# Attention scores in a two-layer trunk: the second pass of the latents' scores on 64 rows, two heads at once

## The chip, the core and the metric

The kernel runs on one core of a Trainium2 chip. A core has a matrix engine (TensorE, "PE" in the profile, with its weight loads as "PEld"), a vector engine (VectorE, "DVE"), an activation engine (ScalarE, "ACT"), GpSimd ("POOL") and a queue that issues DMAs (SyncE, "SP"). The metric is the device time of one execution in microseconds. Before the change it was 1450.35 us, the median of 3 runs (1449.66 to 1453.91).

## The reference

Two layers of a trunk over 512 latent tokens, with a context of 256 tokens that goes through the same weights (the last layer drops the context's own output). Each layer has softmax attention (8 query heads of 64, 2 key heads), gated linear attention (GLA) and a gated MLP over chunks (SGU), merged by gates and normalised. The change is in the attention:

```python
def attend(q, k, v):
    s = jnp.einsum('btgrd,blgd->bgrtl', q, k, preferred_element_type=jnp.float32) * (ATTN_HEAD_DIM ** -0.5)
    p = jax.nn.softmax(s, axis=-1)
    return jnp.einsum('bgrtl,blgd->btgrd', p.astype(v.dtype), v)
...
    k_all = jnp.concatenate([kc, kl], axis=1)
    y_attn = blocked_attention(ql, k_all, v_all) * jax.nn.silu(a_g)
```

A latent query sees 256 + 512 = 768 keys, a context query the 256 of the context. All inputs are float32.

## The kernel before

TensorE takes float32 in a short form (F32R) in one pass, or in full in two. The kernel keeps the precision by splitting a number x into a high part (x rounded to F32R) and a low part (the rest), and by adding up products of the parts. Most matmuls of the kernel are such triples: high by high, high by low, low by high (`mm3`), written as three instructions with 256 to 512 columns.

The scores use the 128 rows of the array in another way. A head has only 64 numbers, so `queries` writes a head's high part and low part side by side (tile `qs`, 128 wide), transposes that (tile `qT`, in which rows 0 to 63 hold the high part and rows 64 to 127 the low part), and the keys' transposed tile `kT` holds each key twice, in the upper and in the lower 64 rows; `kT[:, g, 0]` are the keys' high parts and `kT[:, g, 1]` their low parts. One matmul against `kT[:, g, 0]` then gives (high + low) of the query by the high part of the key; a second one against `kT[:, g, 1]`, which accumulates in the same PSUM tile `s`, adds (high + low) by the low part.

The work is cut into items (t, g, pr): a tile t of 128 queries (t = 0, 1 the context, in layer 0 alone; t = 2 to 5 the latents), a key head g, and a pair pr of the four query heads that share it. For a latent item `scores` takes two PSUM tiles `s` (all there are of that tag), one for each head, and for each head two chunks of keys (512 and 256 columns) by two passes: eight matmuls. Then VectorE takes the negated row maximum (`sm<-s`), ScalarE the exponential with its sum (`P<-s,sm`), VectorE the reciprocal and the product; `values` transposes P on TensorE (`pt<-ident,P`, in full float32), splits it (`PTs`), and multiplies it by the values (`pt<-PTs,V`). There are 4 x 2 x 2 = 16 latent items in each of the two layers, and 8 context items in layer 0.

What stands around it: no engine's order is written by hand. Every operation is recorded with an estimated cost; a list scheduler (`Sched.order`) plays the whole program through with those costs, 16 times with changed priorities, and the order of the shortest plan is issued, engine by engine. So projections of the same layer (rows `p<-...`) are put between the pieces of the attention wherever TensorE would wait, and any changed cost can move instructions anywhere. `sc.group` records several matmuls as one operation with one cost: so far it served the GLA's masks (`s<-M`), 64 x 32 pieces of the array that are addressed by `tile_position`. Some elementwise operations may go to VectorE or GpSimd (`tta`), as the plan finds it cheaper.

Lines of the profile are those of helpers: L421 is the helper that records nearly every operation, L128 the one for operations with a choice of engine, L119 that of `sc.group`. Operations are told apart by their tiles.

Of the kernel before, what the change touches and what calls it, by code (L numbers as in the profile page):

```python
# [10 lines left out]
F32R = mybir.dt.float32r  # L11
I32 = mybir.dt.int32
AF = mybir.ActivationFunctionType
ALU = mybir.AluOpType
# [487 lines left out]
def kernel(ctx: ExitStack, tc: tile.TileContext, A, out, dbg=None):  # L502
    nc = tc.nc
    sc = Sched(nc)
    ACT, DVE, POOL, PE, SP = sc.ACT, sc.DVE, sc.POOL, sc.PE, sc.SP
# [8 lines left out]
    def T(tag, shape, dt=F32, name=None):  # L514
        return sc.tile(sb, shape, dt, tag, BUFS.get(tag, 1), name or tag, "SB")
# [14 lines left out]
    def act(out, in_, func=AF.Copy, **kw):  # L530
        return ACT.activation(out=out, in_=in_, func=func, **kw)
# [12 lines left out]
    def f(ap):  # L544
        return ap.bitcast(F32)
# [5 lines left out]
    identr = C([128, 128], F32R, name="identr")  # L551
# [14 lines left out]
    def tta(out, in0, in1, op):  # L566
        k = dict(out=out, in0=in0, in1=in1, op=op)
        return sc.alt((DVE, "tensor_tensor", k), (POOL, "tensor_tensor", k))
# [19 lines left out]
    LEVELS, SWITCH_PE = [[1, 2], [3, 4], [5, 6], [7]], 87.0  # L588
# [118 lines left out]
    def layer(l, X, start=None):  # L707
# [42 lines left out]
        q = T("T4", [128, 6, 8, 64], name="q")  # L750
        kT = T("T5", [128, 2, 2, NT], F32R, name="kT")
# [78 lines left out]
        for hf in range(2):  # L830
            wt = wgroup(w_in, 8, C_GV + 272 * hf, 272)
            for t in all_t:
                ps = tm(wt, 0, 272, X, t)
# [14 lines left out]
        for w, c0 in ((0, C_GK), (1, C_GQ)):  # L848
            wt = wgroup(w_in, 8, c0, 256)
            for pr in range(2):  # L850
                for seg in (["l", "c"] if (full or w == 0) else ["l"]):
                    ps = cm(wt, 128 * pr, 128, X, seg)
# [24 lines left out]
        for hf in range(2):  # L877
            wt = wgroup(w_in, 8, C_SV + 256 * hf, 256)
            for i, t0 in enumerate((2, 4, 0) if full else (2, 4)):
                g = T("F3", [128, 2, 256], name="keep")  # L880
# [13 lines left out]
        qTs = {}  # L894

        def queries(t, g):
            s = T("Q2", [128, 4, 2, 64], F32R, name="qs")
            act(s[:, :, 0], q[:, t, 4 * g:4 * g + 4])
            tta(s[:, :, 1], q[:, t, 4 * g:4 * g + 4], f(s[:, :, 0]), ALU.subtract)
            ps = PS("pt", [128, 4, 128], F32R)  # L900
            for h in range(4):
                PE.transpose(ps[:, h], s[:, h].rearrange("p a d -> p (a d)"), identr)
            qt = T("Q2", [128, 4, 128], F32R, name="qT")
            act(qt, f(ps))
            qTs[t, g] = qt

        def scores(t, g, pr):

            if pr == 0:
                queries(t, g)  # L910
            nk = (2 if t < 2 else 6) * 128
            sm = T("sm", [128, 16])
            if t < 2:
                S = [PS("s", [128, 2, 256])]
                P = [T("S3", [128, 2, 256], name="P")]
                heads = [(S[0][:, hh], P[0][:, hh]) for hh in range(2)]
            else:
                S = [PS("s", [128, 1, nk]) for _ in range(2)]
                P = [T("S3", [128, 1, nk], name="P") for _ in range(2)]
                heads = [(S[hh][:, 0], P[hh][:, 0]) for hh in range(2)]  # L920
            for hh, (s, p) in enumerate(heads):
                for c0 in range(0, nk, 512):
                    c1 = min(c0 + 512, nk)
                    for w in range(2):
                        PE.matmul(s[:, c0:c1], qTs[t, g][:, 2 * pr + hh], kT[:, g, w, c0:c1], start=(w == 0), stop=(w == 1))
            n = 2 // len(S)
            for i in range(len(S)):
                sc.bias -= SB
                DVE.tensor_reduce(out=sm[:, n * i:n * i + n], in_=S[i], axis=AX.X, op=ALU.max, negate=True)
                sc.bias += SB  # L930
                for hh in range(n * i, n * i + n):
                    act(heads[hh][1], heads[hh][0], AF.Exp, bias=sm[:, hh:hh + 1], accum_out=sm[:, 2 + hh:3 + hh])
                r = sm[:, 4 + n * i:4 + n * i + n]
                DVE.reciprocal(r, sm[:, 2 + n * i:2 + n * i + n])
                if n == 1:
                    sc.alt((DVE, "tensor_scalar", dict(out=P[i][:, 0], in0=P[i][:, 0], scalar1=r, scalar2=None, op0=ALU.mult)),
                           (POOL, "tensor_tensor", dict(out=P[i][:, 0], in0=P[i][:, 0], in1=r.to_broadcast([128, nk]), op=ALU.mult)))
                else:
                    tta(P[i], P[i], r.unsqueeze(2).to_broadcast([128, n, nk]), ALU.mult)
            return [p for _, p in heads]  # L940
# [48 lines left out]
        for grp in DECAYS:  # L989
            eg = {}  # L990
            for d, pr in grp:
                e = T("S3", [128, NT], name="ez")
                g = T("S3", [128, NT], name="gz")
                eg[d, pr] = e, g
                bias = gab[:, d, pr:pr + 1]
                for c0, c1 in ((0, 512), (512, 768)):
                    ps = PS("pt", [128, c1 - c0])
# [5 lines left out]
            for d, pr in grp:  # L1003
                e, g = eg[d, pr]
# [15 lines left out]
        for pr in range(2):  # L1020
# [17 lines left out]
            for c0, c1 in ((0, 4), (4, 6)):  # L1038
                u = PS("s", [128, 2 * (c1 - c0), 128])
                for c in range(c0, c1):  # L1040
# [5 lines left out]
                    for hh in range(2):  # L1046
                        h = 2 * pr + hh
# [4 lines left out]
            for d, seq in ((0, [0, 1, 2, 3, 4, 5]), (1, [1, 0, 5, 4, 3, 2])):  # L1052
                r = slice(64 * d, 64 * d + 64)
# [16 lines left out]
            for gi in range(2):  # L1070
# [4 lines left out]
                for lvs in LEVELS:  # L1075
                    ps = PS("s", [128, 2, 512])
                    calls, kq, views, off, cost = [], [], {}, 0, SWITCH_PE
                    for lv in lvs:
# [23 lines left out]
                        w = 64 if lv in (1, 7) else 32  # L1102
                        views[lv] = ps[:, :, off:off + ng * w].rearrange("p h (c j) -> p h c j", c=ng)
                        off += ng * w
                        for ci in range(ng):
                            for hh in range(2):
                                r = slice(64 * hh, 64 * hh + 64)
# [36 lines left out]
                ps = PS("s", [128, nu, 128])  # L1144
                for j in range(nu):
                    ci, hh = j // 2, j % 2
                    c, h = g0 + ci, 2 * pr + hh
# [67 lines left out]
        for t in q_t:  # L1215
# [7 lines left out]
            ps = PS("pt", [128, 4, 128])  # L1223
# [3 lines left out]
        for b in range(4):  # L1227
            g = T("S3", [128, NQ], name="kept")
# [290 lines left out]
    with tc.manual_schedule():  # L1519
        a = 0  # L1520
# [73 lines left out]
```

## Time and profile before

| | before |
|---|---|
| median of 3 runs | 1450.35 us |
| the profiled execution: its time | 1449.78 us |
| its span on the core | 1448.0 us |
| TensorE busy | 1397.2 us (96%) |
| TensorE weight loads busy | 1232.3 us (85%) |
| VectorE busy | 1041.7 us (72%) |
| ScalarE busy | 664.4 us (46%) |
| GpSimd busy | 140.8 us (10%) |

The span is the time from the first to the last instruction of the profiled execution. A row of the profile has an engine, an operation, its tiles (out<-in), the shape of the weights and of the moving operand, and a count. The busy time of TensorE is from modelled ends: a matmul of 512 columns is listed with 400 ns and the next one starts 0.23 us after it, so what a matmul costs is read from the distance of the starts and not from its duration.

### The profile page before, as it was taken

How to read it: one execution, taken by the hardware profiler on the slowest of the kernel's cores; microseconds unless marked ns; L12 is line 12 of the kernel's file. 1: busy time of each engine (PE TensorE's matmuls, PEld its weight loads, DVE VectorE, ACT ScalarE, POOL GpSimd, SP SyncE). 2: the span in 40 equal slices, each digit the busy share in tenths (PEclk: the TensorE clock that was granted, in tenths of full speed). 3: DMA queues.
4: the chain of work that ended last, by engine and by line, in shares of the span. 5: the costliest groups of instructions: out<-in, count | busy, mean ns of one | idle time of the engine just before them, and what ended most of it. 6: DMA issues, size and time to landing. Idle time of an engine off the chain costs nothing. (4 is left out here: it accounts for less than half of the span.)

```text
span 1448.0 us, 27281 instructions
## 1 busy us (share of the span) xinstructions
PE 1397.2 (96%) x10724; PEld 1232.3 (85%) x10724; DVE 1041.7 (72%) x2252; ACT 664.4 (46%) x1275; POOL 140.8 (10%) x223
## 2 busy tenths in 40 slices
PE   8899999999999999999999999999999879999997
PEld 5798989888888888888889999888977668888887
DVE  8968887998968778422176776898898975433397
ACT  4557666845452224212231365667755443432331
POOL 0031110033310000000000011100023200000003
PEclk9999999999999999999999999999999999999999
DMA  9410002322284554212232332012433265334342
GB/s 323 159 32 19 21 27 65 123 85 71 61 267 152 158 178 143 79 50 73 59 117 88 103 104 62 8 30 74 123 109 91 74 218 175 95 102 109 95 160 95
DMA packets 115890, 151.23 MB, mean 104 GB/s; under 512 B 8601, under 2 KB 89905, under 8 KB 115761
## 3 DMA queue, kind: packets, MB, share of 16 engines
q1 hardware_dynamic: 115762, 149.49, 33.8%
q8 instruction: 84, 1.38, 0.4%
q14 instruction: 44, 0.36, 0.1%
HBM read 134.76 MB, written 14.69 MB: 103 GB/s over the span
## 5 line engine op out<-in xcount | busy, mean ns | idle before, releaser
L128 DVE TENSOR_TENSOR lo<-raw,hi 128x512 fp32r<-128x512 f32 (+1 forms) x295 | 202.9, 695 | 215.5 <-ACT hi L421 206.5
L421 PE MATMUL p<-hlh,hi 128*128 128x512 f32 x704 | 281.6, 400 | 6.1 <-ACT sg L421 3.9
L421 ACT ACTIVATE hi<-raw 128x512 fp32r<-128x512 f32 (+1 forms) x296 | 185.2, 633 | 220.0 <-PE p L421 145.4
L421 PE MATMUL p<-hll,hi 128*128 128x512 f32 x704 | 280.8, 399 | 0.0
L421 PE MATMUL p<-hlh,lo 128*128 128x512 f32 x704 | 280.5, 399 | 0.0
L421 PEld LDWEIGHTS p<-hlh,hi 128*128 128x128 f32 x704 | 132.7, 188 | 34.0 <-ACT sg L421 4.1
L421 PEld LDWEIGHTS p<-hlh,lo 128*128 128x128 f32 x704 | 132.9, 189 | 30.1 <-DVE lo L128 1.1
L421 PEld LDWEIGHTS p<-hll,hi 128*128 128x128 f32 x704 | 132.6, 188 | 26.2
L421 PE MATMUL p<-hch,lo 128*128 128x256 f32 x368 | 104.3, 283 | 0.0
L421 PE MATMUL p<-hcl,hi 128*128 128x256 f32 x368 | 104.3, 283 | 0.0
L421 PE MATMUL p<-hch,hi 128*128 128x256 f32 x368 | 104.2, 283 | 0.0
L421 PE MATMUL p<-hi,hlh 128*128 128x256 f32 (+1 forms) x352 | 101.7, 289 | 0.0
L421 PE MATMUL p<-hi,hll 128*128 128x256 f32 (+1 forms) x352 | 100.5, 286 | 0.0
L421 PE MATMUL p<-lo,hlh 128*128 128x256 f32 (+1 forms) x352 | 99.9, 284 | 0.0
L421 ACT ACTIVATE sig<-p 128x512 f32<-128x512 f32 (+1 forms) x48 | 25.3, 527 | 129.7 <-PE p L421 128.8
L421 POOL TENSOR_SCALAR sf<-sf 128x1 f32<-128x1 f32 x20 | 10.1, 505 | 687.5 <-DVE sf L421 687.0
L421 ACT ACTIVATE P<-s,sm 128x768 f32<-128x768 f32 (+1 forms) x80 | 65.3, 820 | 23.5 <-DVE sm L421 22.9
L421 DVE TENSOR_REDUCE sm<-s 128x1 f32<-128x768 f32 (+1 forms) x72 | 64.8, 921 | 9.6 <-PE s L421 9.5
L421 DVE TENSOR_TENSOR PTs<-pt,PTs 128x512 fp32r<-128x512 f32 x104 | 69.5, 684 | 2.7 <-ACT PTs L421 2.0
L421 PEld LDWEIGHTS p<-hch,hi 128*128 128x128 f32 x368 | 69.5, 189 | 2.0
L421 DVE SCALAR_TENSOR_TENSOR wada<-wada,srow 128x512 f32<-128x512 f32 x96 | 65.5, 689 | 7.7 <-DMA wada<-in_w_adaT_dram 6.3
L421 PEld LDWEIGHTS p<-hcl,hi 128*128 128x128 f32 x368 | 69.3, 188 | 2.1
(296 smaller groups left out, 3386.5 us busy)
## 6 DMA issues: line engine op xcount, KB each, us to landing
raw<-in_w_in_dram SPq DMA_DIRECT2D x204, 256.0 KB, 2.9
wada<-in_w_adaT_dram SPq DMA_DIRECT2D x80, 256.0 KB, 4.5
raw<-in_w_out_dram SPq DMA_DIRECT2D x32, 256.0 KB, 2.9
raw<-in_w_in_dram SPq DMA_DIRECT2D x16, 272.0 KB, 2.9
wada<-in_w_adaT_dram SPq DMA_DIRECT2D x8, 512.0 KB, 5.5
raw<-in_w_br_attn_dram SPq DMA_DIRECT2D x16, 256.0 KB, 3.6
raw<-in_w_br_gla_dram SPq DMA_DIRECT2D x16, 256.0 KB, 3.0
raw<-in_w_br_sgu_dram SPq DMA_DIRECT2D x16, 256.0 KB, 3.0
```

What stands on the lines that cost most here:

```text
L128: fns[p.n] = lambda real=real, k=k: real(**k)
L421: return s.record(n, lambda: real(*a, **k), outs, ins, _cost(n, meth, outs, ins, k), _table(n, k), _dens(n, ins, k), _port(n, meth, outs, ...
```

## The change

The second pass (against the low parts of the keys) of the latent items no longer uses the query's 128 rows (high and low part), but its 64 rows of the high part alone. The two heads of a pair get them in different halves of the array: the layout of `qs` is turned round for every second head, so that head 0 has its high part in rows 0 to 63 and head 1 in rows 64 to 127. The four matmuls of the second pass are recorded as one `sc.group`, alternately of head 0 and head 1, with `tile_position` (0, 0) and (64, 0), at an estimated cost of `SWITCH_PE` (87 ns) and 0.4475 ns for each of 768 columns; the product of the query's low part by the key's low part is left out of the sum. Context items keep both passes.

```diff
@@ queries @@
-            s = T("Q2", [128, 4, 2, 64], F32R, name="qs")
-            act(s[:, :, 0], q[:, t, 4 * g:4 * g + 4])
-            tta(s[:, :, 1], q[:, t, 4 * g:4 * g + 4], f(s[:, :, 0]), ALU.subtract)
+            s = T("Q2", [128, 2, 4, 64], F32R, name="qs")
+            qg = q[:, t, 4 * g:4 * g + 4].rearrange("p (i h) d -> p i h d", i=2)
+            act(s[:, :, 0:4:3], qg)
+            tta(s[:, :, 1:3], qg, f(s[:, :, 0:4:3]), ALU.subtract)
...
-                PE.transpose(ps[:, h], s[:, h].rearrange("p a d -> p (a d)"), identr)
+                PE.transpose(ps[:, h], s[:, h // 2, 2 * (h % 2):2 * (h % 2) + 2].rearrange("p a d -> p (a d)"), identr)
@@ scores @@
+            qt, kh, kl = qTs[t, g], kT[:, g, 0], kT[:, g, 1]
             for hh, (s, p) in enumerate(heads):
                 for c0 in range(0, nk, 512):
                     c1 = min(c0 + 512, nk)
-                    for w in range(2):
-                        PE.matmul(s[:, c0:c1], qTs[t, g][:, 2 * pr + hh], kT[:, g, w, c0:c1], start=(w == 0), stop=(w == 1))
+                    PE.matmul(s[:, c0:c1], qt[:, 2 * pr + hh], kh[:, c0:c1], start=True, stop=False)
+                    if t < 2:
+                        PE.matmul(s[:, c0:c1], qt[:, 2 * pr + hh], kl[:, c0:c1], start=False, stop=True)
+            if t >= 2:
+                calls = []
+                for c0 in range(0, nk, 512):
+                    c1 = min(c0 + 512, nk)
+                    for hh, (s, p) in enumerate(heads):
+                        r = slice(64 * hh, 64 * hh + 64)
+                        calls.append(("matmul", (s[:, c0:c1], qt[r, 2 * pr + hh], kl[r, c0:c1]),
+                                      dict(start=False, stop=True, tile_position=(64 * hh, 0))))
+                sc.group(PE, calls, [s for s, _ in heads], [qt, kl], SWITCH_PE + 0.4475 * nk, 1.0)
```

The order of TensorE's queue, at a latent item of layer 0 whose scores stand in one piece. `s_456` and `s_457` are the PSUM tiles of its two heads, `p_215` is a projection, `pt_464` a transpose for the item two before. Before:

```order
L421 MATMUL p_215<-hi_201,hlh_75 128x272
L421 MATMUL p_215<-lo_202,hlh_75 128x272
L421 MATMUL s_456<-kT_147,qT_454 128x512 x2
L421 MATMUL s_456<-kT_147,qT_454 128x256 x2
L421 MATMUL s_457<-kT_147,qT_454 128x512 x2
L421 MATMUL s_457<-kT_147,qT_454 128x256 x2
L421 MATMUL pt_464<-ident_66,P_435 128x128
```

And with the change:

```order
L421 MATMUL p_215<-hi_201,hlh_75 128x272
L421 MATMUL s_456<-kT_147,qT_454 128x512
L421 MATMUL s_456<-kT_147,qT_454 128x256
L421 MATMUL s_457<-kT_147,qT_454 128x512
L421 MATMUL s_457<-kT_147,qT_454 128x256
L119 MATMUL s_456<-kT_147,qT_454 128x512
L119 MATMUL s_457<-kT_147,qT_454 128x512
L119 MATMUL s_456<-kT_147,qT_454 128x256
L119 MATMUL s_457<-kT_147,qT_454 128x256
L421 MATMUL pt_464<-ident_66,P_435 128x128
```

The eight matmuls over the whole array have become four, with four of 64 rows behind them; the last of head 0 (`s_456`) now stands behind all whole-array matmuls of head 1.

The same queue two items earlier, where the plan takes the scores apart (`s_443` and `s_444` are the two heads, `pt_448` a transpose of P, `pt_437` a product with the values). Before:

```order
L421 MATMUL s_443<-kT_147,qT_431 128x512
L421 MATMUL pt_437<-PTs_412,V_148 128x256 x3
L421 MATMUL s_443<-kT_147,qT_431 128x512
L421 MATMUL s_443<-kT_147,qT_431 128x256 x2
L421 MATMUL s_444<-kT_147,qT_431 128x512 x2
L421 MATMUL s_444<-kT_147,qT_431 128x256 x2
L421 MATMUL pt_448<-ident_66,P_427 128x128
```

And with the change:

```order
L421 MATMUL s_443<-kT_147,qT_431 128x512
L421 MATMUL s_443<-kT_147,qT_431 128x256
L421 MATMUL p_212<-hi_204,hlh_75 128x272
L421 MATMUL pt_437<-PTs_412,V_148 128x256 x3
L421 MATMUL pt_448<-ident_66,P_427 128x128
L421 MATMUL s_444<-kT_147,qT_431 128x512
L421 MATMUL s_444<-kT_147,qT_431 128x256
L119 MATMUL s_443<-kT_147,qT_431 128x512
L119 MATMUL s_444<-kT_147,qT_431 128x512
L119 MATMUL s_443<-kT_147,qT_431 128x256
L119 MATMUL s_444<-kT_147,qT_431 128x256
L421 MATMUL pt_448<-ident_66,P_428 128x128
```

A run of full-float32 transposes (`pt_448`) that stood behind the scores is now cut in two by them.

VectorE's queue at another latent item of layer 0, `s_469` and `s_470` being its heads. Before:

```order
L421 TENSOR_REDUCE sm_468<-s_469 128x1
L421 TENSOR_TENSOR PTs_412<-pt_466,PTs_412 128x512
L421 RECIPROCAL sm_455<-sm_455 128x1
L128 TENSOR_SCALAR P_458<-P_458,sm_455 128x768
L128 TENSOR_SCALAR P_459<-P_459,sm_455 128x768
L421 TENSOR_REDUCE sm_468<-s_470 128x1
```

And with the change:

```order
L421 TENSOR_TENSOR yat_411<-pt_463,ytmp_467 64x128 x2
L421 TENSOR_REDUCE sm_468<-s_469 128x1
L421 TENSOR_TENSOR PTs_412<-pt_474,PTs_412 128x512
L128 TENSOR_TENSOR qs_478<-q_146,qs_478 128x2x128
L421 TENSOR_REDUCE sm_468<-s_470 128x1
```

The maximum of head 0 stands behind more of the older item's work and nearer to that of head 1.

## Rows read from the trace of the kernel before

**Rows 1.** The page: busy time, share of the span and instructions of TensorE and VectorE, and below them the busy tenths of both in 40 equal slices of the span, with TensorE's granted clock in tenths.

```profile
PE 1397.2 (96%) x10724; PEld 1232.3 (85%) x10724; DVE 1041.7 (72%) x2252; ACT 664.4 (46%) x1275; POOL 140.8 (10%) x223
...
PE   8899999999999999999999999999999879999997
...
DVE  8968887998968778422176776898898975433397
...
PEclk9999999999999999999999999999999999999999
```

**Rows 2.** Busy time in stretches (us from the start of the span, length, then busy us and instructions of each engine, granted clock, DMA share, GB/s): layer 0 from the first scores' surroundings to the GLA, its attention alone, and the attention of layer 1.

```profile
70.00:280.00 210.00, 207.37 (x1531) 193.52 (x1529) 174.59 (x359) 146.76 (x318) 27.30 (x32) 1.00 0.17 48
...
93.00:250.00 157.00, 154.37 (x1134) 143.18 (x1133) 133.21 (x271) 106.44 (x248) 21.81 (x21) 1.00 0.13 35
902.00:1006.00 104.00, 101.43 (x717) 92.42 (x716) 90.83 (x185) 71.65 (x156) 6.64 (x7) 1.00 0.13 38
```

**Rows 3.** Who waited for whom, from 70 to 280 us: engine, tile, what it waited for, us in total, times, longest.

```profile
PE pt L421 <- DVE PTs L421: 0.9, 2, 0.5
PE pt L421 <- DVE yat L421: 0.8, 1, 0.8
...
DVE sm L421 <- PE s L421: 4.3, 7, 1.2
```

**Rows 4.** Groups of instructions with their shapes: the scores' matmuls (count, busy us, mean ns).

```profile
L421 PE MATMUL s<-kT,qT 128*128 128x512 f32 x128 | 42.1, 401 | 1.0 <-ACT qT L421 0.7 <-ACT P L421 0.2
L421 PE MATMUL s<-kT,qT 128*128 128x256 f32 x160 | 31.3, 283 | 0.0
```

**Rows 5.** TensorE in order of time around one latent item of layer 0: start us, us, operation, count of merged instructions.

```profile
181.57 0.40 PE L421 MATMUL p<-hll,hi 128*128 128x512 f32 x1
181.81 1.56 PE L421 MATMUL s<-kT,qT 128*128 128x512 f32 x8
183.21 1.04 PE L421 MATMUL pt<-ident,P 128*128 128x128 f32 x8
184.00 0.48 PE L421 MATMUL p<-hlh,lo 128*128 128x512 f32 x1
184.32 0.40 PE L421 MATMUL p<-hlh,hi 128*128 128x512 f32 x1
184.56 0.39 PE L421 MATMUL p<-hll,hi 128*128 128x512 f32 x1
```

**Rows 6.** TensorE in order of time around a group of the GLA's masks, which uses 64 x 32 pieces of the array.

```profile
300.61 0.28 PE L421 MATMUL p<-hcl,hi 128*128 128x256 f32 x1
300.73 0.28 PE L421 MATMUL p<-hch,lo 128*128 128x256 f32 x1
300.85 0.29 PE L421 MATMUL p<-hch,hi 128*128 128x256 f32 x1
301.06 1.02 PE L119 MATMUL s<-M 64*32 64x32 f32 x96
302.01 0.39 PE L421 MATMUL p<-hcl,hi 128*128 128x256 f32 x1
302.24 0.28 PE L421 MATMUL p<-hch,lo 128*128 128x256 f32 x1
302.36 0.28 PE L421 MATMUL p<-hch,hi 128*128 128x256 f32 x1
```

**Rows 7.** The weight loads in that stretch, in order of time, and the loads and matmuls by tile (ns: least, median, most).

```profile
300.61 0.19 PEld L421 LDWEIGHTS p<-hch,lo 128*128 128x128 f32 x1
300.73 0.19 PEld L421 LDWEIGHTS p<-hch,hi 128*128 128x128 f32 x1
301.06 0.91 PEld L119 LDWEIGHTS s<-M 64*32 64x32 f32 x96
302.01 0.19 PEld L421 LDWEIGHTS p<-hcl,hi 128*128 128x128 f32 x1
...
L119 PE MATMUL s<-M x1920: 186/193/241, 297.9 to 1160.8; 64*32 64x32 f32 x160, 64*32 64x64 f32 x32
...
L421 PEld LDWEIGHTS pt<-ident,P x416: 137/140/144, 104.6 to 1018.9; 128*128 128x128 f32 x139
...
L421 PEld LDWEIGHTS s<-kT,qT x288: 186/188/192, 93.4 to 1002.6; 128*128 128x128 f32 x144
```

**Rows 8.** TensorE in order of time, two stretches: the masks' matmuls of 64 columns that start between 314.52 and 314.765 us, and whole-array matmuls of 128 columns in the same full float32.

```profile
314.52 0.46 PE L119 MATMUL s<-M 64*32 64x64 f32 x33 [0.74 <-DVE sf L421]
...
316.58 0.38 PE L421 MATMUL s<-gv,Af 128*128 128x128 f32 x2
316.80 0.39 PE L421 MATMUL s<-St,qx 128*128 128x128 f32 x2
317.03 0.39 PE L421 MATMUL s<-gv,Af 128*128 128x128 f32 x2
```

**Rows 9.** TensorE in order of time around a run of four transposes of P.

```profile
192.56 0.40 PE L421 MATMUL p<-hlh,lo 128*128 128x512 f32 x1
192.79 0.60 PE L421 MATMUL pt<-ident,P 128*128 128x128 f32 x4
193.15 0.48 PE L421 MATMUL p<-hlh,hi 128*128 128x512 f32 x1
193.47 0.40 PE L421 MATMUL p<-hll,hi 128*128 128x512 f32 x1
```

**Rows 10.** VectorE in order of time at the item of rows 5: the maxima of its two heads are the second row.

```profile
182.39 0.43 DVE L128 TENSOR_TENSOR qs<-q,qs 128x256 fp32r<-128x256 f32 x1 [0.41 <-ACT qs L421]
182.73 1.81 DVE L421 TENSOR_REDUCE sm<-s 128x1 f32<-128x768 f32 x2
184.46 0.68 DVE L421 TENSOR_REDUCE sm<-sq 128x8 f32<-128x512 f32 x1
```

## The prediction

> **What bounds the kernel now.** I read the page first: TensorE is busy for 96% of the span, no other engine for more than 72%, and its clock is granted in full in every slice [rows 1]. The stretches say the same of the place that changes: TensorE is busy for 98% of the time from 93 to 250 us (the attention of layer 0) and from 902 to 1006 us (that of layer 1), VectorE for 85% and 87% [rows 2]. The waits confirm it: from 70 to 280 us TensorE waits 1.7 us in all for VectorE, the engine it depends on most [rows 3]. Then I read the order of time, because a busy TensorE need not be one that streams: around a latent item the starts follow each other without a hole [rows 5]. So in both attentions the end moves by what TensorE's queue gets longer or shorter, and the projections that the plan puts between the scores take up any microsecond given back. The question is only what one group of the new kind costs.
>
> **What goes.** Per latent item four of eight matmuls. There are 16 items in each of 2 layers, 32 in all; the counts agree (128 matmuls of 512 columns are 32 x 2 heads x 2 passes; of the 160 of 256 columns 32 belong to the context) [rows 4]. Eight matmuls of an item run from 181.81 to 183.21 us, 1.40 us, so one pass costs 0.70 us [rows 5]. The first pass stays. Removed: 32 x 0.70 = 22.4 us.
>
> **What comes.** If the two heads stream at the same time, the four matmuls of a group take half of 0.70, 0.35 us. Around them stands what the trace shows at the only place where the array already goes from whole to pieces and back, the masks [rows 6].
> - Going in: whole-array matmuls of 256 columns follow each other every 0.12 us; the last one starts at 300.85 and the pieces at 301.06, so 0.21 - 0.12 = 0.09 us pass with nothing started.
> - The first weights: no load is recorded between 300.73 (for the matmul at 300.85) and 301.06 [rows 7], so the first load of a group cannot be hidden. Its price for 128 columns is seen on the way back: the matmul at 302.01, whose load also starts at 302.01, holds up the next one until 302.24, 0.23 instead of 0.12, so 0.11 us. A load of 64 rows has as many columns, and I take the same 0.11; both heads' loads go to different halves, and I let them run together.
> - Going out: the row of 96 ends at 302.08; a mask matmul lasts 0.193 us [rows 7], so the last started at 301.89. Whole-array matmuls of 128 columns in this precision follow every 0.11 us (two in 0.22) [rows 8], so one of 32 columns streams for 0.03 us. From 301.92 to 302.01 are 0.09 us.
> - The next weights, which cannot be loaded ahead either: 0.11 us, as above.
>
> The sum is 0.09 + 0.11 + 0.35 + 0.09 + 0.11 = 0.75 us against 0.70: 0.05 us more, 32 times, +1.6 us. The gain of half the columns is spent on four prices that whole-array matmuls do not pay.
>
> **Corrections from the order.** In the new order 20 of the 32 groups stand before transposes of P; these load in 140 ns where others take 188 [rows 7], so I take 0.05 us off for each, -1.0 us. The plan also cuts runs of these transposes: 138 runs instead of 122. Eight in one run take 0.79 us and make the matmul behind them 0.09 longer (0.32 instead of 0.23), 0.88 together [rows 5]; four take 0.36 and the same 0.09, so two runs of four cost 0.90 [rows 9]. That is 0.02 for each cut, +0.3 us. Net: 1.6 - 1.0 + 0.3 = +0.9 us.
>
> **The bounds of one group.** From below 0.35 us (no drain, every load ahead): 32 x (0.35 - 0.70) = -11.2 us. From above 1.10 us (halves one after the other, all four prices): +12.8 us. I take 0.75, since it is put together from rows of the same switch; what the rows do not show is a load of 64 rows by 128 columns and the F32R form in pieces.
>
> **What is moved and costs nothing.** `queries` has the same 20 roundings and 20 subtractions of 256 numbers and 80 transposes, in other places of the tile; a subtraction takes 0.43 us on VectorE [rows 10], and a longer stride in its operands could add a tenth of that, 0.04 x 20 = 0.8 us, in VectorE's spare time (157 - 133 = 24 us in layer 0, 104 - 91 = 13 us in layer 1 [rows 2]). Without that cover it would be those 0.8 us. The plan has new costs and so a new order nearly everywhere, on SP's and GpSimd's queues too; counted over whole queues, VectorE has 18 instructions fewer and GpSimd 12 more, and from layer 1's decay on TensorE's queue has nearly the same sequence. I give the rest of the order no price of its own, but 3 us to each side in the range.
>
> **A rule against the row.** The Trainium skill, TensorEngine Tiling (Array Packing), "Theoretical Speedup", promises up to 2x where the contraction has 64 rows or fewer. By that alone the sum would be the lower bound of -11.2 us. The same page's "Key Properties" says that a change of the tiling mode drains the engine; the trace agrees, with 0.09 us in and 0.09 us out [rows 6], and it is this that takes the 2x away at groups of only four matmuls.
>
> **Rivals.**
> - A, faster: the switch costs little for pieces that cover all columns, because the drain and the loads hide behind the long streams of 512 columns (the masks stream only 32 or 64). A group then costs what the code notes for it, 0.087 + 0.4475 ns x 768 = 0.43 us: 32 x (0.43 - 0.70) = -8.6 us, less the 0.3 of the cut runs: 1442 us. For it: the load of a whole-array matmul does start one matmul ahead [rows 7]. Against it: that never happens at a switch, in or out [rows 6, 7]. Chance 0.16.
> - B, slower: VectorE takes over. Head 0's maximum used to need the first 0.70 us of an item; now it needs 0.70 + 0.09 + 0.11 + 0.35 = 1.25 us, for the group ends both heads. VectorE is in order, so behind a waiting `sm<-s` stand the splits `PTs` and the products of P, and TensorE's transposes and value products wait for those. The full wait is 0.55 x 32 = 17.6 us; it decides where VectorE's queue arrives before the group's end and has no slack behind. If a third comes through, +5.9 us on top of the 0.9: 1457 us. For it: VectorE's 85%. Against it: its spare 37 us, TensorE's 1.7 us of waiting [rows 3], VectorE's start at 182.73, 0.92 us after the item's first matmul [rows 5, 10], and an order that puts more of the older item ahead of the maximum. Chance 0.14.
> - C, slower, the change does not do what it says: the halves stream one after the other in F32R. +0.35 x 32 = 11.2 us more: 1462 us. Against it: 33 mask matmuls of 64 columns start within 0.245 us; each streams for half of 0.11 us, 1.8 us together, so with the last stream's 0.055 some six were under way at once [rows 8], where one half of the array has room for four of 32 columns. Chance 0.07.
> - D, slower than forecast: the second load of a head (for its 256 columns) waits for the end of that head's 512 columns, since it is for the same rows. +0.11 us a group, 3.5 us: 1455 us. For whole-array matmuls the trace shows the opposite: the load at 300.73 runs while the matmul that started at 300.73 streams through the same rows [rows 6, 7]. No row shows it for 64 rows. Chance 0.08. The Trainium skill, TensorE: Matmul & The Clock Gate, Part 3 ("The mechanism"), has this as its rule for packed matmuls: a load overlaps a running matmul only in another group of rows.
>
> **How the numbers follow.** The profiled execution took 1449.78 us (its span of 1448.0 and 1.8 around it), 0.57 below the median. 1449.78 + 0.9 = 1450.7 against it; against the median 1450.35 + 0.9 = 1451.2. I predict 1451 us, no measurable change. My case has the chance 0.55 and its own range from 1447 to 1456 us: 0.03 us more or less in any two of the four prices is 2 us over 32 groups, and the order has its 3. About 0.3%, 4.35 us, is what a measurement of this kernel can tell from no change, so the borders are 1446.0 and 1454.7. My case gives 0.05 faster, 0.42 same, 0.08 slower; A 0.14 faster, 0.02 same; B 0.02 same, 0.12 slower; C 0.07 slower; D 0.04 and 0.04. Together 0.19 faster, 0.50 same, 0.31 slower. The range from 1443 to 1459 us takes in B and D and half of A, and leaves out C and the end of A, some 0.18.
>
> **What will show it.** In the new trace the four matmuls of L119 that write `s`: the two of 512 columns must start within some 0.02 us of each other (else C), the first one 0.09 us late behind the whole-array matmul ahead of it, and from the start of the group to the start of what follows some 0.55 us, with the matmul behind holding up its successor by 0.11. If the loads of a group start before the whole-array matmul ahead has ended, A holds; if a head's two matmuls lie 0.11 us further apart than its 512 columns need, D. If VectorE's waits for `s` grow from 4.3 us in layer 0 to over 10, and TensorE's for `PTs` with them, B. I am wrong altogether if TensorE's idle time grows or shrinks by more than 4 us outside the two attentions, which would be the order's doing.

## The result: 0.5% slower, and the profile after

The changed kernel takes 1458.76 us (median of 6 runs, 1455.86 to 1463.87), the kernel before on the same chip 1451.32: ratio 1.0053, 95% interval 1.0031 to 1.0075. A second measurement gave 1458.59 us and 1.0054 [1.0041, 1.0066]. The forecast was 1451 us and no measurable change; it is slower by more than 0.3%. The profiled execution is the slowest of the six (1463.87 us), and its mean granted clock the lowest (0.988; the others 0.990 to 0.993), so its spans are some 5 us longer than the median's; that of before lies 1.5 us below its median. Of the 14.1 us between the two spans (1462.1 and 1448.0) only 7.4 are thus the change in the medians.

The page's busy line, to [rows 1], and the attention of layer 0, to [rows 2]:

```profile
PE 1403.1 (96%) x10724; PEld 1228.0 (84%) x10724; DVE 1034.5 (71%) x2234; ACT 667.2 (46%) x1281; POOL 159.4 (11%) x235
```

```profile
93.00:250.00 157.00, 153.62 (x1139) 138.04 (x1138) 129.93 (x266) 108.16 (x251) 27.05 (x25) 1.00 0.13 35
```

Both look as before. So does the place of the change. TensorE in order of time around one latent item, to [rows 5]:

```profile
179.68 0.28 PE L421 MATMUL p<-hch,hi 128*128 128x256 f32 x1
179.79 0.85 PE L421 MATMUL s<-kT,qT 128*128 128x512 f32 x4
180.58 0.62 PE L119 MATMUL s<-kT,qT 64*128 64x512 f32 x4
181.13 1.09 PE L421 MATMUL pt<-ident,P 128*128 128x128 f32 x8
181.98 0.36 PE L421 MATMUL p<-hcl,hi 128*128 128x256 f32 x1
182.18 0.28 PE L421 MATMUL p<-hch,lo 128*128 128x256 f32 x1
```

The same view for a narrow window alone, 180.57 to 180.60 us (a row is what runs in it, the count what has begun by its end); the weight loads, first those that have begun by 180.62 us, then those by 180.75; and the 512-column matmuls of all groups, to [rows 4]:

```profile
180.37 0.28 PE L421 MATMUL s<-kT,qT 128*128 128x256 f32 x1
180.58 0.51 PE L119 MATMUL s<-kT,qT 64*128 64x512 f32 x2
```

```profile
180.58 0.19 PEld L119 LDWEIGHTS s<-kT,qT 64*128 64x128 f32 x2 [0.24 <-issue]
...
180.58 0.30 PEld L119 LDWEIGHTS s<-kT,qT 64*128 64x128 f32 x4 [0.24 <-issue]
```

```profile
L119 PE MATMUL s<-kT,qT 64*128 64x512 f32 x64 | 16.0, 497 | 0.0
```

How to read it: two matmuls of 0.497 us each have begun by 180.60 and take 0.51 us together, so the two heads stream side by side. The last whole-array matmul starts at 180.37 and takes 0.12 us of the stream [rows 6]; the group starts at 180.58: 0.09 us with nothing started. The group lasts to 181.13, 0.55 us. Behind it the eight transposes take 0.85 us to the start of the next matmul, where they took 0.79 [rows 5]: 0.06 us for the load that could not run ahead. Together 0.70 us here, ahead of transposes, and 0.75 where a projection follows: the one at 94.87 us is followed 0.24 us later, the next one 0.12 us later.

Where, then, does the time go? The instructions of three tiles (count, ns least/median/most, first and last start) serve as milestones: the value products `pt<-PTs,V` of the first and the second layer, the SGU's transposes `pt<-sgc,sv` and the projections `p<-ysh,hi` of layer 0. Before, then after:

```profile
L421 PE MATMUL pt<-PTs,V x224: 274/283/387, 109.0 to 251.1; 128*128 128x256 f32 x112
L421 PE MATMUL pt<-sgc,sv x48: 270/275/348, 433.8 to 442.4; 128*128 128x128 f32 x48
L421 PE MATMUL p<-ysh,hi x64: 274/335/398, 729.5 to 762.6; 128*128 128x512 f32 x32, 128*128 128x256 f32 x32
L421 PE MATMUL pt<-PTs,V x192: 277/283/388, 909.2 to 1021.4; 128*128 128x256 f32 x192
```

```profile
L421 PE MATMUL pt<-PTs,V x224: 274/282/386, 108.5 to 251.3; 128*128 128x256 f32 x112
L421 PE MATMUL pt<-sgc,sv x48: 271/275/347, 445.4 to 454.2; 128*128 128x128 f32 x48
L421 PE MATMUL p<-ysh,hi x64: 274/335/398, 746.5 to 779.6; 128*128 128x512 f32 x32, 128*128 128x256 f32 x32
L421 PE MATMUL pt<-PTs,V x192: 274/283/388, 923.0 to 1037.8; 128*128 128x256 f32 x192
```

Layer 0's attention ends 0.2 us later. From there to the SGU's transposes, the GLA of layer 0, 11.4 us are lost (194.1 against 182.7), to `ysh` 5.4 more (301.1 against 295.7). From `ysh` to the end of layer 1's attention 0.6 are won (291.3 against 291.9), and 2.3 behind it. That is the 14.1 us between the two spans. None of the new groups stands in the two stretches that lose. TensorE's waits from 252 to 470 us, before and after (tile, what it waited for, us in total, times, longest):

```profile
PE pt L421 <- DVE o L421: 1.5, 1, 1.5
PE s L119 <- DVE Ac L421: 1.3, 1, 1.3
...
PE s L119 <- DVE M L128: 0.9, 2, 0.5
```

```profile
PE s L119 <- DVE M L128: 6.8, 3, 3.0
PE s L119 <- DVE Ac L421: 4.0, 3, 1.4
PE pt L421 <- DVE sv L128: 2.7, 1, 2.7
```

All waits of that stretch sum to 6.6 us before and 15.0 after. The longest, in order of time on each engine:

```profile
404.70 1.45 DVE L421 COPY Af<-s 32x192 f32<-32x192 f32 x4
408.61 0.69 DVE L128 TENSOR_TENSOR lo<-raw,hi 128x512 fp32r<-128x512 f32 x1 [2.46 <-ACT hi L421]
409.34 0.96 DVE L128 TENSOR_TENSOR M<-M,qk 128x768 f32<-128x768 f32 x1
```

```profile
407.95 0.63 ACT L421 ACTIVATE hi<-raw 128x512 fp32r<-128x512 f32 x1 [5.47 <-DMA raw<-in_w_in_dram]
408.48 0.83 ACT L421 ACTIVATE M<-M 128x768 f32<-128x768 f32 x1
```

```profile
407.01 0.40 PE L421 MATMUL p<-hlh,lo 128*128 128x512 f32 x1
410.45 0.96 PE L119 MATMUL s<-M 64*32 64x64 f32 x48 [3.03 <-DVE M L128]
```

TensorE wants the last masks M. VectorE could make them, but ahead of them in its queue stands the split `lo` of a weight block; that waits for ScalarE's `hi`, which waits 5.47 us for the block's transfer, and ScalarE's part of the masks stands behind it. The transfer was late by the order too: SyncE's queue (its waits from 375 to 412 us, then its next issues) had stood 15.3 us for a buffer that an earlier `lo` frees.

```profile
SPq L421 <- DVE lo L128: 17.2, 3, 15.3
```

```profile
402.67 0.97 SPq L421 DMA_DIRECT2D raw<-in_w_in_dram  x2
```

And after the wait TensorE's clock is at half, its lower level of 1.2 GHz, from 410 to 415 us, and at 0.83 on average from 415 to 420. It is not the only such place. Stretches before, then after (the clock is the third number from the end):

```profile
252.00:455.00 203.00, 195.99 (x2478) 171.85 (x2477) 180.42 (x374) 107.18 (x176) 46.43 (x69) 1.00 0.40 122
```

```profile
410.00:415.00 5.00, 4.55 (x59) 3.84 (x60) 0.30 (x1) 1.56 (x3) 0.00 (x0) 0.50 0.89 277
300.00:360.00 60.00, 55.02 (x844) 48.94 (x835) 51.48 (x111) 27.55 (x51) 22.40 (x36) 0.97 0.23 69
360.00:430.00 70.00, 63.21 (x976) 54.24 (x975) 52.16 (x108) 32.75 (x52) 19.70 (x30) 0.93 0.41 130
520.00:600.00 80.00, 77.47 (x432) 67.04 (x431) 60.60 (x159) 24.16 (x47) 0.00 (x0) 0.98 0.50 153
```

Before, the clock is full (1.00) from 252 to 455 us and from 455 to 900. After, it falls behind four waits of TensorE: 1.95 us for `M` at 313.77, 1.84 us for `M` at 384.91, the 3.03 us shown, and 2.22 us for the tile `mac` at 576.56, in the stretch up to `ysh`. (Behind the 2.7 us for `sv` it does not fall.) By the three longer stretches this is worth up to 60 x 0.03 + 70 x 0.07 + 80 x 0.02 = 8.3 us of TensorE's time (an estimate; it counts in full only where TensorE is the bound), of the 16.8 us lost up to `ysh` in this execution.

The theory was therefore: the halves are neutral, as forecast, and the time is lost by the order in which the plan has come out, in waits and in the lower clock behind them. The rival: the halves cost it, by the joint end of both heads or by something that their place does not show.

### The profile page after: what moved, and what is told of

It reads as the page before. It is cut to its first block, busy times and chain, and to the rows that moved or that the text cites. A ratio compares the mean times of both kernels' runs of the same rounds, so it can differ in the third digit from the quotient of the medians.

```text
span 1462.1 us, 27270 instructions
## 1 busy us (share of the span) xinstructions
PE 1403.1 (96%) x10724; PEld 1228.0 (84%) x10724; DVE 1034.5 (71%) x2234; ACT 667.2 (46%) x1281; POOL 159.4 (11%) x235
## 5 line engine op out<-in xcount | busy, mean ns | idle before, releaser
L421 POOL TENSOR_SCALAR sf<-sf 128x1 f32<-128x1 f32 x20 | 6.9, 344 | 728.6 <-DVE sf L421 728.0
L421 ACT ACTIVATE PTs<-pt 128x512 fp32r<-128x512 f32 x104 | 61.5, 599 | 36.3 <-PE pt L421 33.8
```

Source lines behind the costliest of these rows:

```text
L421: return s.record(n, lambda: real(*a, **k), outs, ins, _cost(n, meth, outs, ins, k), _table(n, k), _dens(n, ins, k), _port(n, meth, outs, ...
```

## The experiments

**1. The halves in the order of before.** The plan gets the eight matmuls of before; each item's last one is replaced by the group of halves, and what reads head 0's scores is held until then.

```diff
-        for i in seq:
-            fn = self.ops[i][1]
-            (fn[self.gone[i]] if isinstance(fn, dict) else fn)()
+        for i in emit(self, seq):
...
+        met[g[0]] += 1
+        if met[g[0]] == len(g):
+            second_(self, self.calls[g[0]])
+            done.update(g)
```

> The plan is that of the kernel before, its order kept instruction by instruction; only the second pass of each latent item is emitted as four matmuls of 64 rows at the place of the last second-pass matmul before, and what needs head 0's score is held until then. If the order is what cost the 7.4 us (theory: order), a group costs 0.05 us more than the pass it replaces and the time is that of before, 1451 to 1453 us. If the halves themselves cost it (rival: the switch, the joint end of both heads, VectorE's waits), it stays at about 1458 us.

Measured: 1480.06 us, ratio 1.0196 [1.0183, 1.0210]. Neither number. VectorE's and ScalarE's waits in layer 1's attention, before (890 to 1025 us) and here (900 to 1055 us; the groups are on L573):

```profile
DVE sm L421 <- PE s L421: 5.2, 9, 1.2
...
ACT P L421 <- DVE sm L421: 12.7, 10, 2.2
```

```profile
DVE sm L421 <- PE s L573: 14.8, 15, 1.7
...
ACT P L421 <- DVE sm L421: 36.4, 17, 3.1
```

The whole loss stands in the two attentions. The milestones of above are 10.0 us late at the end of layer 0's attention, 10.2 at the SGU, 11.0 at `ysh`, and 29.7 at the end of layer 1's attention, which the span keeps (1477.7 against 1448.0). So the order of before costs next to nothing (0.2 and 0.8 us) where the changed kernel loses 11.4 and 5.4. But an order laid out for two heads that end one after the other is bad for two that end together.

**2. Whole-array matmuls in the order of the changed kernel.** All five queues as in the changed kernel, only the four second matmuls use the whole array.

```diff
-  calls.append(("matmul", (s[:, c0:c1], qt[r, 2 * pr + hh], kl[r, c0:c1]),
-                dict(start=False, stop=True, tile_position=(64 * hh, 0))))
+  calls.append(("matmul", (s[:, c0:c1], qt[:, 2 * pr + hh], kl[:, c0:c1]),
+                dict(start=False, stop=True)))
```

> The plan and the order of the changed kernel, the same on all five queues, but the second pass is four whole-array matmuls again, with no switch. Theory order: within 2 us of the changed kernel, about 1458 us, since 0.70 us replaces 0.70 to 0.75. Rival halves: back to 1451 us.

Measured: 1457.64 us, 1.0037 [1.0025, 1.0050]. Against before in the same session 5.6 us are there without the halves, where the changed kernel loses 7.4. The halves cost 1.1 us by the medians, 1.8 if each kernel is taken against its own before; the intervals overlap, so this cannot be told from nothing.

**3. A truer price told to the plan.** The code notes 0.43 us for a group that takes 0.70 to 0.75; 0.29 us are added.

```diff
-  sc.group(PE, calls, [s for s, _ in heads], [qt, kl], SWITCH_PE + 0.4475 * nk, 1.0)
+  sc.group(PE, calls, [s for s, _ in heads], [qt, kl], SWITCH_PE + 0.4475 * nk + 290, 1.0)
```

> The changed kernel with 0.72 us noted for a group in place of 0.43, and so a new order everywhere; what the group does is the same. Theory order: any time that an order can give, 1447 to 1460 us, and a different one from 1458.8 by more than 1 us; if a plan with the right price is a better plan, 1451 us or less. Rival halves: 1458 us again.

Measured: 1463.13 us, 1.0078 [1.0066, 1.0090]. That lies outside the 1447 to 1460 us expected of an order. A truer price made a worse order, so the wrong price by itself is not the cause.

**4. No second pass at all.** The order of the changed kernel without the groups.

```diff
-  PE.matmul(s[:, c0:c1], qt[:, 2 * pr + hh], kh[:, c0:c1], start=True, stop=False)
+  PE.matmul(s[:, c0:c1], qt[:, 2 * pr + hh], kh[:, c0:c1], start=True, stop=t >= 2)
...
-  sc.group(PE, calls, [s for s, _ in heads], [qt, kl], SWITCH_PE + 0.4475 * nk, 1.0)
+  calls = []
+  sc.group(PE, calls, [s for s, _ in heads], [qt, kl], SWITCH_PE + 0.4475 * nk, 1.0)
```

> The plan and the order of the changed kernel, with the second pass left out altogether (the scores lack the product with the keys' low parts). Theory order, with TensorE as the bound in both attentions: 32 x 0.70 to 0.75 us = 22 to 24 us less than the changed kernel, 1435 to 1437 us. If VectorE bounds the attention (rival B of the prediction), much of that does not reach the end: 1445 us or more.

Measured: 1442.62 us, 0.9936 [0.9923, 0.9949], 16.1 us below the changed kernel. The value products and TensorE's waits from 70 to 280 us:

```profile
L421 PE MATMUL pt<-PTs,V x224: 277/282/389, 107.2 to 246.9; 128*128 128x256 f32 x112
```

```profile
PE pt L421 <- DVE PTs L421: 4.3, 9, 1.4
```

Layer 0's attention ends 4.4 us earlier (246.9 against 251.3), though 16 groups of 0.70 us, 11.2 us, are gone. TensorE now waits for VectorE's splits 9 times instead of the changed kernel's 3 (4.3 us against 2.3). So even a second pass for nothing would give back less than half of its TensorE time here. All of TensorE's waits from 70 to 252 us grow by 3.2 us (6.4 against 3.2); the rest of the missing 6.8 was not followed. From `ysh` to the end of layer 1's attention 6.9 of another 11.2 us come through (284.4 against 291.3), and the median of 16.1 lies between the two answers expected, 22 to 24 us and under 14. The profiled execution is the slowest of its kernel (1450.69 us), so its stretches are read one by one and not as a sum.

**5 and 6. The instructions of before, planned with other prices.** Each is the kernel before. In 5 (first line added) the price noted for the 128 matmuls of the latents' second pass is multiplied by 0.431/0.697; in 6 (second line, in its place) that of all 256 score matmuls of the latents is 1 ns higher:

```diff
-  PE.matmul(s[:, c0:c1], qTs[t, g][:, 2 * pr + hh], kT[:, g, w, c0:c1], start=(w == 0), stop=(w == 1))
+  i = PE.matmul(s[:, c0:c1], qTs[t, g][:, 2 * pr + hh], kT[:, g, w, c0:c1], start=(w == 0), stop=(w == 1)); sc.ops[i] = sc.ops[i][:4] + (sc.ops[i][4] * (0.431 / 0.697 if t >= 2 and w else 1),) + sc.ops[i][5:]
...
+  i = PE.matmul(s[:, c0:c1], qTs[t, g][:, 2 * pr + hh], kT[:, g, w, c0:c1], start=(w == 0), stop=(w == 1)); sc.ops[i] = sc.ops[i][:4] + (sc.ops[i][4] + (1.0 if t >= 2 else 0.0),) + sc.ops[i][5:]
```

> The instructions of the kernel before, each head by itself; only the noted cost of the latents' second-pass matmuls is lowered so that an item's four make 0.43 us, as the change notes for a group. If the loss comes from the wrong price in the plan, this loses what the changed kernel loses: 1457 to 1460 us. If it needs the joint end of both heads, it stays near 1451 us. If any new order loses, it lies between 1452 and 1463 us with no link to the price.

> The instructions of the kernel before with 1 ns more noted for each of the latents' score matmuls (256 instructions, 0.3 us in all): a new order from nothing. Theory any order: not 1451 us but some 1453 to 1462 us, lost in the second half of layer 0's GLA and behind it. Rival (the loss comes from what the change notes): 1451 us within 2.

Measured: 1458.48 us, 1.0041 [1.0027, 1.0055], and 1458.01 us, 1.0045 [1.0031, 1.0058]. One nanosecond in the plan's prices costs 6.5 us, about as much as the change, without the change. Each order loses at its own places, though. Between the milestones, 5 loses 4.2 us up to the end of layer 0's attention, 5.7 in the GLA and 4.0 up to `ysh`. The loss of 6 was expected from the second half of the GLA on; it is 1.1 us in the GLA, 3.7 up to `ysh` and 2.9 from there to the end of layer 1's attention.

**7 and 8. Two more orders.** Seven: 2 with the whole-array group noted at what it takes (0.697 us). Eight: 6 with 1 ns less instead of more.

```diff
-  sc.group(PE, calls, [s for s, _ in heads], [qt, kl], SWITCH_PE + 0.4475 * nk, 1.0)
+  sc.group(PE, calls, [s for s, _ in heads], [qt, kl], 0.9075 * nk, 1.0)
```

> Whole-array second pass recorded as one group of both heads, at its right price of 0.70 us. If the joint end of the heads is what spoils the plan, this loses as the changed kernel does, 1457 to 1463 us, mostly inside the attentions; if the wrong price is, it is back at 1451 us; if any new order loses, somewhere between 1452 and 1463 us.

> As the run with 1 ns more, with 1 ns less for each of the latents' score matmuls: another new order from nothing. Theory any order: 1452 to 1462 us, and another value than with 1 ns more. Rival: 1451 us within 2.

Measured: 1450.97 us, 0.9993 [0.9980, 1.0005], and 1450.49 us, 0.9992 [0.9981, 1.0004]. Neither can be told from before. Seven also shows that a joint end of both heads need not cost anything in all once the order is planned for it (layer 0's attention ends 2.0 us later, at 253.1 us; from `ysh` to the end of layer 1's attention 0.5 us are won).

**9. The halves in the order of 7.** The edit of 7's price alone, in the changed kernel; all queues as in 7.

> The changed kernel, its second pass in the halves as before, but the price that the plan is told for it is that of whole-array matmuls (0.9075 ns per key, 0.697 us for 768 keys, instead of 0.431 us). By this the order on every queue is the one of e7, which ran at 1450.97 us with whole-array matmuls. If the order alone made the changed kernel slow, and the halves cost what the pair of the changed kernel and e2 showed (+1.1 us, 0.70 to 0.75 us a group against 0.70), this takes 1451 to 1453 us, ratio 1.000 to 1.002. If the halves themselves cost the 7 us wherever they stand, it takes 1457 to 1459 us.

Measured: 1453.74 us, 1.0014 [1.0002, 1.0026]. Five of the seven us are gone, and by the interval it is within 0.3% of before. The halves cost 2.8 us against 7. Run 3 has the same instructions with 0.72 us noted for a group instead of 0.70, and takes 9.4 us more.

**10. Whole-array matmuls in the held order of 1.**

```diff
-  second.append((i, c0, hh, (s[:, c0:c1], qTs[t, g][r, 2 * pr + hh], kT[r, g, 1, c0:c1])))
+  second.append((i, c0, hh, (s[:, c0:c1], qTs[t, g][:, 2 * pr + hh], kT[:, g, 1, c0:c1])))
...
-  sc.calls[second[0][0]] = [(x[3], dict(start=False, stop=True, tile_position=(64 * x[2], 0)))
+  sc.calls[second[0][0]] = [(x[3], dict(start=False, stop=True))
```

> The order of e1 on every queue (the order of the kernel before, with the second passes of both heads of a pair together at the place of the later one, and what reads head 0's scores held until then), with whole-array matmuls in the place of the halves. If e1's 28 us came from the joint end of both heads in an order that was planned for separate ends (VectorE and ScalarE get head 0's scores about 0.7 us later, and head 1's in the same moment), this takes 1477 to 1481 us, as e1 did (1480.06). If the halves caused them, it takes 1450 to 1454 us.

Measured: 1482.72 us, 1.0224 [1.0206, 1.0241]. The loss of experiment 1 is the joint end in an order that was not made for it, not the halves; these are even 2.7 us faster here. They give the scores some 0.15 us earlier (0.55 against 0.70), and VectorE's waits for them are 1.0 us less in all; the rest of the 2.7 was not followed.

**11. Two pairs of neighbours exchanged.** In the changed kernel, at the wait of 3.03 us read above: on ScalarE `M<-M` ahead of `hi<-raw`, on VectorE `M<-M,qk` ahead of `lo<-raw,hi`. TensorE's, GpSimd's and SyncE's queues are as they were. The numbers are the plan's operations, the first of each pair set behind the second:

```diff
-        for i in seq:
+        for i in moved(seq, ((3929, 3764), (3930, 3765))):
```

> The changed kernel with two neighbours exchanged on ScalarE and two on VectorE, all else in its order: in layer 0's GLA the last masks (M<-M on ScalarE, M<-M,qk on VectorE) now stand ahead of the split of a weight block (hi<-raw, lo<-raw,hi), which waits there for a late transfer. If an order's loss lies in such places, TensorE's wait of 3.0 us for M at 410.45 us shrinks to under 0.8 us (the weight block itself is wanted next, and its two halves are ready 0.7 us before the masks were), the clock stays full behind it (in the changed kernel it fell to 0.50 from 410 to 415 us and 0.83 to 420, which is some 3 us more), and the time falls by 2 to 6 us, to 1453 to 1457 us. If what is saved here is lost again at the next wait, or the loss lies elsewhere, it stays at 1458 to 1459 us.

Measured: 1455.42 us, 1.0027 [1.0016, 1.0037]. VectorE's and TensorE's rows at the same place:

```profile
403.30 0.98 DVE L128 TENSOR_TENSOR M<-M,qk 128x768 f32<-128x768 f32 x1
405.12 0.69 DVE L128 TENSOR_TENSOR lo<-raw,hi 128x512 fp32r<-128x512 f32 x1 [0.84 <-ACT hi L421]
```

```profile
404.15 0.40 PE L421 MATMUL p<-hlh,lo 128*128 128x512 f32 x1
404.48 0.72 PE L119 MATMUL s<-M 64*32 64x64 f32 x48
```

```profile
410.00:415.00 5.00, 5.00 (x32) 4.24 (x30) 1.38 (x2) 1.51 (x2) 1.52 (x2) 1.00 1.00 368
415.00:420.00 5.00, 2.25 (x11) 1.84 (x11) 4.01 (x6) 4.99 (x9) 0.00 (x0) 0.85 1.00 365
```

TensorE does not wait for these masks any more, and its clock is full from 410 to 415 us. But a new wait stands close behind: at 417.87 us TensorE waits 2.75 us for the tile `o`, and the clock falls there (0.85 from 415 to 420).

**12. The changed kernel once more**, beside 11.

> The changed kernel itself once more, on the same chip as the run with the two swaps, so that these can be compared: 1456 to 1461 us if its first measurement (1458.76 us) holds, and in its profile again the first scores to the last value product of layer 0 within 1 us of the kernel before, and the start of the SGU's transposes in layer 0 9 to 12 us later than there.

Measured: 1458.59 us, so the two exchanges are worth 3.2 us (the intervals of the two ratios do not meet). Its value products and its wait at the masks:

```profile
L421 PE MATMUL pt<-PTs,V x224: 274/282/388, 109.1 to 251.9; 128*128 128x256 f32 x112
L421 PE MATMUL pt<-sgc,sv x48: 272/275/422, 443.9 to 454.4; 128*128 128x128 f32 x48
```

```profile
410.83 0.71 PE L119 MATMUL s<-M 64*32 64x64 f32 x48 [1.52 <-DVE M L128]
```

The GLA loses 9.3 us here as well (192.0 from the last value product to the SGU's transposes, against 182.7 before). The wait at the masks is half as long here, 1.52 us, and no lower clock follows it, so the 3.2 us are the price of this order of neighbours, but not of the very wait and clock of the first profile. With the exchange the SGU's transposes start at 438.8 us:

```profile
L421 PE MATMUL pt<-sgc,sv x48: 273/275/348, 438.8 to 447.6; 128*128 128x128 f32 x48
```

None of the versions that compute everything beats before by more than can be measured.

## Why the prediction was wrong

- **The price of a group** held: 0.09 in, 0.11 + 0.35 + 0.09 as 0.55 in one piece (its three terms are not seen apart), 0.11 behind (0.06 ahead of transposes). By itself +0.9 us was forecast; in the same order the halves cost +1.1 us (changed kernel against 2), +2.8 (9 against 7) and -2.7 (1 against 10). The two intervals of a pair make each of these differences uncertain by some 2.5 to 4 us. The first two agree with the forecast; the third does not quite, and why the halves are faster there stays open.
- **Rival A**, drain and loads hidden: the loads start with the group, at 180.58, not before. A group costs 0.70 to 0.75 us against 0.70. The "Theoretical Speedup" of up to 2x in the Trainium skill, TensorEngine Tiling (Array Packing), is there in the streaming (0.51 us for two matmuls of 0.497), and the drain of its "Key Properties" (0.18 us in and out) takes it away together with the loads that cannot run ahead (0.22 us, 0.17 ahead of transposes); the drain alone, as the prediction has it, would not.
- **Rival C**, halves one after the other: no, by the same two rows.
- **Rival D**, the second loads wait: no. The second pair of loads begins 0.11 us after the group (0.30 less the 0.19 of one load) and runs under the first two matmuls, which by their modelled ends last to 0.51; the group's 0.55 us leave no room for a second 0.11. Part 3 ("The mechanism") of the Trainium skill's TensorE: Matmul & The Clock Gate says in its list of what overlaps that a load does so only with a matmul in other rows; these rows go against that sentence. They fit the second case that the same section of the Trainium skill names, a load into the background weight buffer.
- **Rival B**, both heads end late: did not happen in the changed kernel. From 70 to 280 us VectorE waited 3.9 us for scores (the two rows below; 4.3 before [rows 3]); the sign I had named was over 10. The mechanism exists, at some 28 us where I had put 5.9, when the order is not planned for it (experiments 1 and 10); planned for, it cost nothing that can be measured (7).

```profile
DVE sm L421 <- PE s L119: 2.6, 3, 1.6
DVE sm L421 <- PE s L421: 1.3, 3, 0.9
```

- **"So in both attentions the end moves by what TensorE's queue gets longer or shorter"** was too strong. Taking 11.2 us out of TensorE's queue in layer 0 moved the end of its attention by 4.4: by the listed waits, VectorE is the next bound, a few us below. In layer 1 it was 6.9 of 11.2. (TensorE's waits for VectorE before were 2.0 us from 70 to 280 us, not the 1.7 that I had added up: 0.3 for the tile `qs` belong to them.) It did no harm here, since the change moved TensorE's time by so little; rival A's price would have come out too large.
- **"its clock is granted in full in every slice [rows 1]"** read more than the row says: a 9 stands for 90% or more, and before the clock was already 0.97 from 1060 to 1240 us. The sum had no term for the clock. In the changed kernel's profile it is worth up to some 8 us between 300 and 600 us; the clocks of its other five executions are higher.
- **The step that failed** is "I give the rest of the order no price of its own, but 3 us to each side in the range". The mechanism was named (TensorE's idle time outside the attentions, "which would be the order's doing") and is what happened, but the term was mis-sized. Read from the whole time against before, it measures from -1 us (8) to +7 (5, 6) with the very instructions of before, and with the halves, their own cost included, from +2 (9) to +11 (3). In the changed kernel it is +5.6 (2). Here it is a knot of queues that are served in order: a weight split ahead of the masks, a transfer issued late behind a buffer, and a lower clock after the wait. The exchange of two pairs of neighbours gave 3.2 us of it back, which shows that the order at this place costs time; how much of it is the wait and how much the clock is not shown. The other places (the earlier waits for `M`, those for `Ac` and `sv`, and the wait for `mac` in the stretch up to `ysh`) are read from the trace and were not tried.
- **The queries' new layout** costs nothing, as said: a subtraction on VectorE takes 0.43 us before and after (median), without the tenth that I had allowed for its longer stride.

The time of 1458.8 us lies at the upper edge of the range (1459), and outside the likeliest case's own (1456). I had put 0.31 on slower, for rivals B, C and D and a little of my own case; it came by none of the rivals.

## What to carry to other kernels

Where a planner sets the order, a small change to its prices draws a new order, and that draw can outweigh the edit: measure its spread first (the old instructions with a price off by 1 ns), or run the edit and its opposite in the same order, before an edit is credited or blamed. Packing two products into the array's halves halves their stream, but each switch costs a drain and a load that nothing hides, 0.4 us in and out here (0.09 + 0.11 twice), so by this estimate a group must replace more than 0.8 us of whole-array streaming before half of it is worth the switch. And an engine that is busy for 98% of a stretch can have a second engine a few us behind it.

## What the runs showed of the hardware

Two 64-row matmuls in F32R of 512 columns run side by side (0.51 us for both, 0.497 for one), and 64-row loads for the same rows run under them (the rows at 180.58 us). After the wait of 3.03 us TensorE's clock stood at 0.50 for 5 us; in the second profile of the same kernel, after 1.52 us at the same place, that stretch shows it full:

```profile
410.00:415.00 5.00, 4.17 (x73) 3.84 (x74) 0.68 (x1) 1.57 (x3) 0.00 (x0) 1.00 0.82 260
```
